# Adding the experts' rows to their tokens by indirect DMA with addition, in place of one-hot products

## The chip, the cores and the metric

The kernel runs on one core of one Trainium2 chip. The metric is device time in microseconds (us) of one execution. The runs before the change took 3098.67 us in the median of three (3094.47 to 3103.86).

## The reference

A two-layer transformer block on 512 tokens of width 1024 with a second, "context" stream of 256 tokens, and then one hybrid layer on the main stream. All is in float32. In each of the two layers both streams pass attention and convolution mixers and then a mixture of 16 experts; the second layer needs the main stream only. The experts choose their tokens:

```python
cap = CAPACITY_FACTOR * t // N_EXPERTS        # 64 rows of the main stream, 32 of the context
gates, idx = lax.top_k(jnp.swapaxes(aff, 1, 2), cap)
xs = jax.vmap(lambda hb, ib: hb[ib])(h, idx)
y = jnp.einsum('becf,efd->becd', jax.nn.silu(a) * u, w_down)
y = y * gates[..., None].astype(y.dtype)
return jax.vmap(lambda ib, yb: jnp.zeros((t, d), yb.dtype).at[ib.reshape(-1)].add(yb.reshape(-1, d)))(idx, y)
```

So every expert's 64 (or 32) output rows of 1024 numbers, times a gate, are added to the tokens that it chose (`x_new + g2 * ...`, with one row of gains g2 for all tokens). A token can be chosen by several experts, and by one expert once.

## The kernel before, in words

The stage that changes is `moe` of the first layer with its loop `experts_two`. A stands for the main stream (4 tiles of 128 tokens, `cap` 64, `dup` 2), B for the context (2 tiles, `cap` 32, `dup` 4). `dup` says how a row of 1024 is cut so that an expert's rows fill 128 partitions: two halves of 512 numbers for A, four quarters of 256 for B.

Before the loop, `out_proj` leaves each stream's rows in on-chip tiles `x` and `xc`; `route_tile` (L1068) norms each tile of 128 tokens, stores it to a tensor `xd` in memory on ScalarE's DMA queue, and works out the routing; `route_turn` leaves, for each expert, a column of row numbers `gi` and a column of gates `ig`.

In the loop over 16 experts, TensorE's instructions stand in the order in which the program writes them (`manual_schedule` over MAN, which is PE); the other engines are ordered by the tile framework. For one expert TensorE does: products of A's gathered rows with the up and gate weights (L1203, 64 instructions), transposes of the next rows of A (L1185), the same products for B (L1203, 128 instructions, on narrower tiles), transposes of the activations (L1224), then the down products of A and of B (L1240, 32 and 64 instructions). The rows are gathered by indirect DMAs on GpSimd (`gather`, L1171) four experts ahead. The weights, 12 entries of 1 MiB for an expert, come on SyncE's DMA queue (L227) into a ring of 13 buffers: an entry is loaded when the buffer that it takes has been read by both streams.

`expert_down` writes the gated rows (down product times gate times g2, on VectorE, L1246) into a tile Y in which the rows of `dup` experts gather: two experts of A or four of B fill it. `combine` (L1249) then adds Y to the tokens: it builds a one-hot matrix from the row numbers on VectorE (L1258), splits Y into a high and a low part (L306 on ScalarE, L307 on VectorE or GpSimd), multiplies with the one-hot matrix on TensorE (L1281: 16 products of 512 columns for A, 8 for B) and adds the result to `x` or `xc` on VectorE (L1284). It is a generator; its pieces are put between the B products of the next expert at the places listed in `PAT` (L1328). The last blocks of both streams have no next expert, and run after the loop. Then `x` stays on chip for the second layer's first norm, and a copy `xsave` is stored to memory, which the second layer reads back later (L980).

`row_bcast` (L388) spreads g2 over all partitions with products (L394) and two copies. In the first expert it does so for A and B, between two groups of weight products. The second layer's loop, `experts_one`, has one stream and calls `combine` with halves of Y. Its first norm (`norm_T`: squares on ScalarE L298, a scale on VectorE, scaled rows L333 and L335, transposes L339) reads `x` directly.

Of the kernel before, what the change touches and what calls it, by code (L numbers as in the profile page):

```python
# [64 lines left out]
CV = 1  # L65
# [24 lines left out]
# columns of the constant array  # L90
# [10 lines left out]
# columns of the row array, read by every partition  # L101
# [12 lines left out]
class Kern:  # L114
# [65 lines left out]
    def load_consts(self):  # L180
# [7 lines left out]
        # sinks negated  # L188
# [28 lines left out]
    def issue(self):  # L217
# [6 lines left out]
        if self.behind is not None:  # L224
            # the load is to queue up behind the rows that are needed before it
# [38 lines left out]
    def rsqrt(self, v, w):  # L264
        """1/sqrt(v) for [128, w], by Newton's steps"""
# [12 lines left out]
    def rsqrt1(self, v):  # L278
        """1/sqrt(v) for [128, 1], by Newton's steps that leave out powers of two until the last"""
# [12 lines left out]
    def rms_scale(self, xs):  # L292
        """per token 1/rms of tiles [128, 1024]"""
# [9 lines left out]
    def split(self, src, hi, lo, eng=None):  # L303
        """hi + lo = src, each with no more bits than one pass carries"""
# [4 lines left out]
    def evac(self, out, in_):  # L309
        """copy out of PSUM, on the two engines in turn"""  # L310
# [12 lines left out]
    def norm_T(self, src, dst, nt, acol, bcol, hi, lo, r=None):  # L323
        """(rms-normed rows)^T * a + b, split, [128 d, 8, tokens]; dst(t) takes the normed rows, hi(k), lo(k) the result"""
# [23 lines left out]
    def mods_steps(self, rounds):  # L348
        """thirds of the modulation vectors, on the partitions; an entry of the stream for each step"""
# [29 lines left out]
    def affine(self, l, m, which):  # L379
        """gain * (1 + scale) on the partitions, for the first (0) or the second (1) norm"""  # L380
# [6 lines left out]
    def row_bcast(self, vec, out, halves=None):  # L387
        """vec [128, 8] on the partitions as a row on every partition"""  # L388
# [27 lines left out]
    def rounds(self, l):  # L416
        """thirds of the modulation that are worked out beside the projections of layer l"""
# [47 lines left out]
    def load_x(self, src, srcc, eng=None):  # L465
        """the residual stream, [128 tokens, tiles, 1024]"""
# [28 lines left out]
    def layer(self, l):  # L495
# [6 lines left out]
        # normed inputs, transposed  # L502
# [60 lines left out]
        # the last layer has room for some of the experts' weights early  # L563
# [15 lines left out]
    def two(self, hT, w, m, n):  # L579
        """two groups of 128 channels"""  # L580
# [9 lines left out]
    def long_conv(self, l, hT, y, sets):  # L590
        """the conformer's convolution"""
# [5 lines left out]
        for ch in range(2):  # L597
            w = self.take_hl(dve=WDVE)
            for m, n in sets:
# [9 lines left out]
                # taps on the vector engine, and (all of the second stream's) on the scalar engine and the pool engine  # L609
# [19 lines left out]
    def channel_norm(self, l, y, sets):  # L629
        """layer norm over the convolution's channels, and silu"""  # L630
# [59 lines left out]
    def att_tiles(self, last):  # L690
        """turned queries of both streams, turned keys of both kinds, and values"""
# [4 lines left out]
    def key_tiles(self):  # L696
        """turned keys of both kinds: the high parts, on both halves of the partitions, and the low ones"""
# [3 lines left out]
    def early_T(self, T, tiles):  # L701
        """the normed inputs turned while the modulation is still on its way, in tiles that attention needs later"""
# [23 lines left out]
    def qkv_group(self, l, hT, last, tiles, W):  # L726
# [85 lines left out]
                # the turning of a tile comes after the products of the next two  # L812
# [13 lines left out]
    def soft(self, ps, n, scale, sink=None, lam=None, pool=None):  # L826
        """softmax of two heads' scores, sink negated; with lam the first less lam times the second"""
# [34 lines left out]
    def pT(self, P, n):  # L862
        """two heads' probabilities transposed: [128 keys, chunks, 2 heads x 128]"""
# [24 lines left out]
    def q_stack(self, q, kind, n):  # L888
        """a block's queries split, the low parts on the other half of the partitions"""
# [9 lines left out]
    def scores(self, out, qs, kT, kv, g, a, b, last=True):  # L899
        """one head's scores of keys a to b"""  # L900
# [71 lines left out]
    def out_proj(self, l, y, T, slots):  # L972
        """x + gate * (y @ w_out), and every tile of it through the second norm and the router"""
# [35 lines left out]
        # by columns first, the first columns' weights make room for the experts'  # L1009
# [3 lines left out]
        for i, t, h in order:  # L1013
# [3 lines left out]
            # the channels that are done last come last  # L1017
# [9 lines left out]
            # the routing of a tile comes after the next products  # L1027
# [21 lines left out]
    def route_init(self, l, m, nt):  # L1049
        """what the router needs: its weights with the gain of the norm in them, and the shift's part of its sums"""  # L1050
# [9 lines left out]
        for k in range(8):  # L1060
# [4 lines left out]
                    xd=self.dram.tile([n, 1024], F32, name=self.nm("xd")),  # L1065
                    wk=[self.one(self.rk, (w,), s=f"wk{m}{w}") for w in (n, 257)], best=[])

    def route_tile(self, l, R, t, x):  # L1068
        """a tile's second norm, stored for the gathers, and its affinities, transposed"""
        nc = self.nc  # L1070
        # the second stream's tiles end beside the first experts, so they take other banks
# [30 lines left out]
        nc.scalar.dma_start(out=R["xd"][t * 128:(t + 1) * 128, :], in_=xs)  # L1102

# [955 lines left out]
```

## Time and profile before

| | |
|---|---|
| time of the runs, median (lowest to highest) | 3098.67 us (3094.47 to 3103.86) |
| profiled execution: span (its only time) | 3111.6 us |
| busy: PE, PEld, DVE, ACT, POOL | 94%, 59%, 45%, 27%, 14% of the span |
| mean granted clock of TensorE | 0.971 |
| DMA | 612.67 MB, mean 197 GB/s |

PE is TensorE's products, PEld its weight loads beside them, DVE VectorE, ACT ScalarE, POOL GpSimd, SP SyncE. The profile's L numbers are the lines of the kernel before. A granted clock of 1.00 is 2.4 GHz, 0.50 is 1.2 GHz. A row of the timeline gives start and length in us, engine, line, operation, the tiles written and read, the number of instructions and, in brackets, idle time before it and what ended it. The first layer's experts lie between about 507 and 1114 us, the second layer's between about 1475 and 1945 us.

### The profile page before, as it was taken

The page shows a single profiled execution, that of the slowest core. Times are in us where ns is not written, and L with a number is a line of the kernel's source. Part 1 is how long each engine was busy: PE and PEld are TensorE (multiplying, and loading weights), DVE is VectorE, ACT ScalarE, POOL GpSimd, SP SyncE. Part 2 cuts the span into 40 slices and gives each one's busy share as a digit, 9 for nine tenths or more (in the row PEclk, how much of TensorE's full clock was granted, in tenths as well). Part 3 has the DMA queues.
Part 4 walks back from the last instruction along what each step waited for, and adds up shares of the span by engine and source line. Part 5 has one row for each costly group of instructions (what it writes and reads, how often), then busy time and mean ns, then how long its engine had stood idle before and what let it go on. Part 6 is the DMA issues. An engine that isn't in the chain of part 4 may idle for free.

```text
span 3111.6 us, 39027 instructions
## 1 busy us (share of the span) xinstructions
PE 2928.2 (94%) x15824; PEld 1831.4 (59%) x15824; DVE 1402.5 (45%) x2893; ACT 847.9 (27%) x1565; POOL 437.2 (14%) x371
## 2 busy tenths in 40 slices
PE   6989999999999989997998888999999999999998
PEld 3556775444444456565332222787887767788786
DVE  4478754232323266765222222642437563354344
ACT  4256431000000143652000000421235442332122
POOL 2224232000000031432000000221210000200000
PEclk9989989999999999898999999999999999999999
DMA  7710126999988844036999999232231112222222
GB/s 269 268 57 14 42 88 248 379 376 359 353 336 338 335 150 177 14 125 235 404 409 409 409 409 390 70 106 84 90 118 62 55 68 81 102 95 95 92 91 75
DMA packets 147236, 612.67 MB, mean 197 GB/s; under 512 B 10416, under 2 KB 10544, under 8 KB 129136
## 3 DMA queue, kind: packets, MB, share of 16 engines
q1 hardware_dynamic: 138272, 580.82, 48.8%
q10 hardware_dynamic: 5040, 17.55, 1.5%
q0 software_dynamic: 3744, 11.81, 1.2%
q8 instruction: 125, 2.05, 0.3%
q14 instruction: 55, 0.45, 0.0%
HBM read 598.60 MB, written 11.53 MB: 196 GB/s over the span
## 4 chain that ended last, share of the span: by engine, by line
PE 70%; DMA 7%; DVE 5%; issue 1%; ACT 1%; POOL 0%; DVEq 0%; POOLq 0%; ACTq 0%
PE pb L1203 11%; PE pd L1240 8%; PE pd L319 7%; PE pd L320 7%; PE pd L321 7%; PE pd L1203 4%; DMA w<-w_up 4%; PE pb L319 3%; PE pb L320 3%; PE pb L321 3%; PE pa L319 3%; PE pa L320 3%; PE pa L321 3%; DMA w<-w_down 2%; PE pb L1281 1%; PE pb L1272 1%
## 5 line engine op out<-in xcount | busy, mean ns | idle before, releaser
L1203 PE MATMUL pb<-w,X 128*64 128x512 f32 x2048 | 466.5, 599 | 26.6 <-DMA w<-w_up 16.6
L1203 PEld LDWEIGHTS pb<-w,X 128*64 128x64 f32 x2048 | 149.2, 137 | 326.4 <-issue 255.7
L258 ACT CAST wh<-w 128x1024 fp32r<-128x1024 f32 (+3 forms) x239 | 236.1, 1029 | 366.2 <-issue 124.6
L1240 PE MATMUL pd<-w,hT 128*64 128x512 f32 (+1 forms) x2048 | 304.3, 494 | 7.9 <-DMA w<-w_down 2.9
L259 DVE TENSOR_TENSOR wl<-w,wh 128x1024 fp32r<-128x1024 f32 (+2 forms) x187 | 229.2, 1244 | 141.4 <-ACT wh L258 136.5
L319 PE MATMUL pd<-hh,wh 128*128 128x512 f32 (+1 forms) x720 | 285.3, 397 | 8.0 <-ACT wh L258 3.3
L321 PE MATMUL pd<-hh,wl 128*128 128x512 f32 (+1 forms) x720 | 283.8, 394 | 0.2 <-DVE wl L259 0.2
L320 PE MATMUL pd<-hl,wh 128*128 128x512 f32 (+1 forms) x720 | 283.5, 394 | 0.0
L259 POOL TENSOR_TENSOR wl<-w,wh 128x1024 fp32r<-128x1024 f32 (+1 forms) x52 | 134.8, 2593 | 482.5 <-ACT wh L258 467.4
L1240 PEld LDWEIGHTS pd<-w,hT 128*64 128x64 f32 (+1 forms) x2048 | 102.5, 124 | 167.4 <-issue 132.0
L1213 ACT ACTIVATE s<-pb 128x512 f32<-128x512 f32 x32 | 19.1, 598 | 640.8 <-PE pb L1203 640.8
L319 PEld LDWEIGHTS pd<-hh,wh 128*128 128x128 f32 x720 | 138.4, 192 | 39.9 <-ACT wh L258 6.3
L321 PEld LDWEIGHTS pd<-hh,wl 128*128 128x128 f32 x720 | 138.1, 192 | 30.0 <-DVE wl L259 1.7
L320 PEld LDWEIGHTS pd<-hl,wh 128*128 128x128 f32 x720 | 138.7, 193 | 27.0 <-issue 0.2
L1191 DVE TENSOR_TENSOR X<-pa,aff 128x512 f32<-128x512 f32 (+1 forms) x48 | 28.9, 602 | 274.8 <-PE pa L1185 274.5
L1246 DVE SCALAR_TENSOR_TENSOR Y<-pd,ig,g 64x512 f32<-64x512 f32 (+1 forms) x128 | 78.7, 615 | 161.7 <-PE pd L1240 160.1
L319 PE MATMUL pb<-wh,fh 128*128 128x512 f32 x352 | 139.3, 400 | 0.8 <-DVE x L1626 0.8
L320 PE MATMUL pb<-wl,fh 128*128 128x512 f32 x352 | 139.3, 396 | 0.0
L321 PE MATMUL pb<-wh,fl 128*128 128x512 f32 x352 | 139.2, 396 | 0.0
L319 PE MATMUL pa<-hh,wh 128*128 128x512 f32 x352 | 139.0, 395 | 0.0
L320 PE MATMUL pa<-hl,wh 128*128 128x512 f32 x352 | 139.0, 395 | 0.0
L321 PE MATMUL pa<-hh,wl 128*128 128x512 f32 x352 | 139.0, 395 | 0.0
(456 smaller groups left out, 4941.4 us busy)
## 6 DMA issues: line engine op xcount, KB each, us to landing
w<-w_up SPq DMA_DIRECT2D x128, 1024.0 KB, 18.5
w<-w_gate SPq DMA_DIRECT2D x128, 1024.0 KB, 12.6
w<-w_down SPq DMA_DIRECT2D x128, 1024.0 KB, 15.9
w<-ada_w SPq DMA_DIRECT2D x48, 1024.0 KB, 6.7
w<-w_in SPq DMA_DIRECT2D x18, 1024.0 KB, 7.7
w<-f1g SPq DMA_DIRECT2D x11, 1024.0 KB, 4.9
w<-f1u SPq DMA_DIRECT2D x11, 1024.0 KB
w<-f2g SPq DMA_DIRECT2D x11, 1024.0 KB, 4.9
```

Source lines behind the costliest of these rows:

```text
L258: nc.scalar.copy(hi[:, s], w[:, s])
L259: (nc.gpsimd if i and not (dve or self.dve) else nc.vector).tensor_tensor(lo[:, s], w[:, s], hi[:, s].bitcast(F32), op=ALU.subtract)
L319: nc.tensor.matmul(ps, lhsT=l[0], rhs=r[0], start=first, stop=False)
L320: nc.tensor.matmul(ps, lhsT=l[0], rhs=r[1], start=False, stop=False)
L321: nc.tensor.matmul(ps, lhsT=l[1], rhs=r[0], start=False, stop=last)
L1191: nc.vector.tensor_tensor(Xv, pv, bc(R["A"]), op=ALU.mult)
L1203: nc.tensor.matmul(pp[h * cap:(h + 1) * cap, 0:w], lhsT=X[:, k], rhs=Wk[:, h * w:(h + 1) * w], start=(k == 0), stop=(k == 7))
L1213: nc.scalar.activation(out=s, in_=pp[:, 0, 0:w], func=AF.Silu)
L1240: nc.tensor.matmul(py[h * cap:(h + 1) * cap, 0:w], lhsT=hT[:, k % nj, k // nj], rhs=Wd[k // 2][:, k % 2, h * w:(h + 1) * w], start=(k == 0 ...
L1246: nc.vector.scalar_tensor_tensor(Y[o:o + cap, h * w:(h + 1) * w], py[sl, 0:w], R["ig"][sl, 16 + e:17 + e], g2[sl, h * w:(h + 1) * w], op0= ...
L1272: nc.tensor.matmul(ps[:, t], lhsT=oh[:, (2 * t2 + t) * 128:(2 * t2 + t + 1) * 128], rhs=z[:, i], start=(i == 0), stop=(i == 1))
L1281: nc.tensor.matmul(ps[:, h * 512:(h + 1) * 512], lhsT=oh[:, t * 128:(t + 1) * 128], rhs=yh[h][:, i], start=(i == 0), stop=(i == 1))
```

## The change

In the first layer the one-hot products go. Each stream gets a tensor `sum` in memory; every tile of tokens is stored there by `route_tile`, in addition to `xd`. Each expert's gated rows are written to a fresh tile Y of 128 partitions in one VectorE instruction per stream (before: one for each half or quarter), and an indirect DMA on GpSimd's queue adds them to the chosen rows of `sum`, with the same row numbers `gi` as the gather. g2 is kept folded in the same way (`fold`). Behind the loop both streams are loaded from `sum` on ScalarE's queue, and `sum` of the main stream takes the place of `xsave`. The second layer keeps its one-hot products; its `combine` loses the branches that it did not use. Comments and docstrings are dropped, too (not shown).

```diff
@@ route_init
+                    sum=self.dram.tile([n, 1024], F32, name=self.nm("sum")) if l == 0 else None,
@@ route_tile
         nc.scalar.dma_start(out=R["xd"][t * 128:(t + 1) * 128, :], in_=xs)
+        if l == 0:
+            nc.scalar.dma_start(out=R["sum"][t * 128:(t + 1) * 128, :], in_=x)
@@ expert_down
-        per = dup
-        o = (e % per) * cap
-        for h in range(dup):
-            sl = slice(h * cap, (h + 1) * cap)
-            nc.vector.scalar_tensor_tensor(Y[o:o + cap, h * w:(h + 1) * w], py[sl, 0:w], R["ig"][sl, 16 + e:17 + e],
-                                           g2[sl, h * w:(h + 1) * w], op0=ALU.mult, op1=ALU.mult)
+        out(py)
+
+    def scatter(self, R, e, g2):
+        nc = self.nc
+        dup = R["dup"]
+        w = 1024 // dup
+        def f(py):
+            Y = self.one(self.yp, (w,), s=f"Y{R['m']}", bufs=2)
+            nc.vector.scalar_tensor_tensor(Y, py[:, 0:w], R["ig"][:, 16 + e:17 + e], g2, op0=ALU.mult, op1=ALU.mult)
+            nc.gpsimd.indirect_dma_start(
+                out=R["sum"].rearrange("t (h w) -> (t h) w", h=dup),
+                out_offset=bass.IndirectOffsetOnAxis(ap=R["gi"][:, e:e + 1], axis=0), in_=Y, in_offset=None, compute_op=ALU.add)
+        return f
+
+    def fold(self, R, row, out):
+        dup, cap = R["dup"], R["cap"]
+        w = 1024 // dup
+        for h in range(dup):
+            sl = slice(h * cap, (h + 1) * cap)
+            self.nc.scalar.copy(out[sl], row[sl, h * w:(h + 1) * w])
@@ experts_two
-            pieces = (None for f in pend for _ in f)
-            pend = []
-            next(pieces, None)
...
+                row = self.one(self.yp, (1024,), s="g2")
                 for r, g in zip(R, g2):
-                    self.row_bcast(self.mod(l, r["m"], 5), g)
+                    self.row_bcast(self.mod(l, r["m"], 5), row)
+                    self.fold(r, row, g)
...
-                if i in PAT:
-                    next(pieces, None)
...
-            self.expert_down(A, e, h0, Wd, Y[0], g2[0], lambda: h1.append(self.expert_T(B, s1)))
-            self.expert_down(B, e, h1[0], Wd, Y[1], g2[1])
+            self.expert_down(A, e, h0, Wd, self.scatter(A, e, g2[0]), lambda: h1.append(self.expert_T(B, s1)))
+            self.expert_down(B, e, h1[0], Wd, self.scatter(B, e, g2[1]))
             self.rel(4)
-            for r in R:
-                if e % r["dup"] == r["dup"] - 1:
-                    pend.append(self.combine(r, e, Y[r["m"]], [self.xc] if r["m"] else self.x, False))
-        return pend
@@ moe
-                pend = self.experts_two(R, g2, l)
+                self.experts_two(R, g2, l)
+            self.xsave = R[0]["sum"]
+            self.load_x(self.xsave, R[1]["sum"])
...
-        if l == 0:
-            self.xsave = self.dram.tile([512, 1024], F32, name="xsave")
-            for t in range(4):
-                nc.scalar.dma_start(out=self.xsave[t * 128:(t + 1) * 128, :], in_=self.xt(t))
```

## Rows read from the trace of the kernel before

**Rows 1.** The page: the span, and busy tenths in 40 slices of it.

```profile
span 3111.6 us, 39027 instructions
...
PE   6989999999999989997998888999999999999998
...
DMA  7710126999988844036999999232231112222222
```

**Rows 2.** Stages: stretch, its us, busy us of five engines, clock, DMA share, GB/s.

```profile
507.70:513.50 5.80, 5.80 (x15) 1.72 (x16) 5.22 (x22) 0.47 (x1) 0.56 (x2) 0.50 0.96 354
549.93:583.67 33.74, 33.74 (x304) 13.81 (x301) 8.38 (x16) 2.81 (x5) 3.11 (x3) 1.00 1.03 408
583.67:622.46 38.79, 38.79 (x320) 16.08 (x316) 11.61 (x17) 1.57 (x3) 2.00 (x3) 1.00 0.90 350
656.20:696.93 40.73, 40.73 (x328) 17.57 (x324) 16.85 (x24) 2.71 (x5) 3.34 (x4) 1.00 0.96 364
549.93:1096.24 546.31, 546.31 (x4634) 226.88 (x4630) 165.55 (x270) 40.51 (x71) 34.53 (x32) 1.00 0.90 349
1096.24:1117.68 21.44, 14.37 (x45) 6.58 (x41) 15.08 (x31) 8.40 (x16) 5.17 (x3) 0.68 0.43 155
1510.00:1860.00 350.00, 306.70 (x1340) 111.19 (x1336) 87.64 (x115) 18.11 (x30) 9.53 (x10) 1.00 1.03 409
```

**Rows 3.** The same for the one-hot products alone (L1281): PE, PEld, then clock.

```profile
549.93:1096.24 546.31, 40.63 (x136) 22.87 (x136) 1.00 0.90 349
```

**Rows 4.** Groups by line and shape, 545 to 1100 us: busy us, mean ns.

```profile
L1246 DVE SCALAR_TENSOR_TENSOR Y<-pd,ig,g 64x512 f32<-64x512 f32 x32 | 24.0, 750 | 42.0 <-PE pd L1240 41.6
...
L1171 POOL DMA_INDIRECT gat<-xd,gi x20 | 19.2, 958 | 279.7 <-PE pa L1185 279.7
```

**Rows 5.** DMA from 537 to 600 us: all; issues, KB, median us to landing.

```profile
DMA packets 6698, 25.68 MB, mean 408 GB/s; under 512 B 441, under 2 KB 441, under 8 KB 6694
...
w<-w_gate SPq DMA_DIRECT2D x5, 1024.0 KB, 15.7
gat<-xd,gi POOLq DMA_INDIRECT x4, 6.2
```

**Rows 6.** Timeline of SyncE: an issue of the weight stream.

```profile
571.44 2.11 SPq L227 DMA_DIRECT2D w<-w_gate  x1
```

**Rows 7.** Timeline of TensorE and ScalarE, first expert.

```profile
507.40 0.37 PE L1098 MATMUL pb<-ct,aff 128*16 128x128 f32 x1 [3.45 <-DVE aff L1095]
...
529.14 1.16 PE L394 MATMUL pa<-ct,mods 128*128 128x128 f32 x8 [1.02 <-DVE g L315]
...
530.13 0.60 PE L1185 MATMUL pa<-ct,gat 128*128 128x128 f32 x4
...
529.15 0.59 ACT L313 COPY g<-pa 128x512 f32<-128x512 f32 x1 [2.24 <-PE pa L394]
```

**Rows 8.** DMA from 440 to 480 us, all queues.

```profile
DMA packets 435, 1.61 MB, mean 40 GB/s; under 512 B 48, under 2 KB 48, under 8 KB 432
```

**Rows 9.** Timeline of TensorE around the end of the last expert.

```profile
1085.12 3.65 PE L1240 MATMUL pd<-w,hT 128*64 128x512 f32 x16
...
1089.07 7.25 PE L1240 MATMUL pd<-w,hT 128*64 128x512 f32 x80
1096.24 0.50 PE L1281 MATMUL pb<-Yh,oh 128*128 128x512 f32 x1
...
1117.68 1.28 PE L339 MATMUL pa<-ct,x 128*128 128x128 f32 x8 [0.22 <-DVE x L335]
```

**Rows 10.** Line L471, loads of a stream's tiles of 512 KB.

```profile
DMA to landing us min/median/max: 3.4/5.2/8.8
```

**Rows 11.** Timeline of ScalarE: the squares and scaled rows behind the experts.

```profile
1111.40 1.06 ACT L298 ACTIVATE junk<-x 128x1024 bf16<-128x1024 f32 x1
1112.36 0.19 ACT L298 ACTIVATION_READ_ACCUMULATOR junk<-x 128x1 f32 x1
...
1117.13 2.56 ACT L333 ACTIVATE x<-x,rsy 128x512 f32<-128x512 f32 x4 [0.85 <-DVE rsy L275]
```

More of the change, by code (lines that the diff above doesn't have):

```diff
@@ L1227, in expert_T, with expert_down @@
         return hT
-    def expert_down(self, R, e, hT, Wd, Y, g2, beside=None):
+    def expert_down(self, R, e, hT, Wd, out, beside=None):
         nc = self.nc
@@ L1258, in combine @@
             nc.vector.tensor_scalar(oh[sl], self.iota[sl, :n], R["ig"][sl, ee:ee + 1], None, op0=ALU.is_equal)
-        yh = []
         for h in range(2):
             c = slice(h * 512, (h + 1) * 512)
-            z = self.one(self.yp, (2, 512), F32R, "Yh", bufs=1 if halves else YHB)
-            self.split(Y[:, c], z[:, 0], z[:, 1], (nc.vector, nc.gpsimd)[h and not (CV and halves)])
-            yh.append(z)
-            if h and not halves:
-                yield
-            if halves or YHB == 1:
-                for t2, xs in enumerate(src):
-                    ps = self.pb((2, 512))
-                    for t in range(2):
-                        for i in range(2):
-                            nc.tensor.matmul(ps[:, t], lhsT=oh[:, (2 * t2 + t) * 128:(2 * t2 + t + 1) * 128], rhs=z[:, i],
-                                             start=(i == 0), stop=(i == 1))
-                    nc.vector.tensor_tensor(xs[:, :, c], xs[:, :, c], ps, op=ALU.add)
-                    yield
-        if not (halves or YHB == 1):
-            for t in range(nt):
-                ps = self.pb()
-                for h in range(2):
+            z = self.one(self.yp, (2, 512), F32R, "Yh", bufs=1)
+            self.split(Y[:, c], z[:, 0], z[:, 1], (nc.vector, nc.gpsimd)[h and not CV])
+            for t2, xs in enumerate(src):
+                ps = self.pb((2, 512))
+                for t in range(2):
                     for i in range(2):
-                        nc.tensor.matmul(ps[:, h * 512:(h + 1) * 512], lhsT=oh[:, t * 128:(t + 1) * 128], rhs=yh[h][:, i],
+                        nc.tensor.matmul(ps[:, t], lhsT=oh[:, (2 * t2 + t) * 128:(2 * t2 + t + 1) * 128], rhs=z[:, i],
                                          start=(i == 0), stop=(i == 1))
-                xs = src[t // 2][:, t % 2]
-                nc.vector.tensor_tensor(xs, xs, ps, op=ALU.add)
+                nc.vector.tensor_tensor(xs[:, :, c], xs[:, :, c], ps, op=ALU.add)
                 yield
     def experts_two(self, R, g2, l):
-        nc = self.nc
         A, B = R
-        Y = [None, None]
-        pend = []
         X = [self.gather_T(A)]
@@ L1296, in experts_two @@
             Wu, Wg = [], []
-            pieces = (None for f in pend for _ in f)
-            pend = []
-            next(pieces, None)
             for k in range(8):
@@ L1327, in experts_two @@
                 self.expert_mm(B, X[1], lambda k: (Wu, Wg)[b][k // 2][:, k % 2], p[:, 1 - b], [k])
-                if i in PAT:
-                    next(pieces, None)
                 if i == TAT:
                     h0 = self.expert_T(A, s0)
-            for _ in pieces:
-                pass
             self.rel(8)
@@ L1400, in moe @@
         ey = self.phase(yp=1)
-        self.iota = self.one(self.yp, (512,), s="iota")
-        nc.gpsimd.iota(self.iota, pattern=[[1, 512]], base=0, channel_multiplier=0, allow_small_or_imprecise_dtypes=True)
-        g2 = [self.one(self.yp, (1024,), s=f"g2{r['m']}") for r in R]
+        if l == 1:
+            self.iota = self.one(self.yp, (512,), s="iota")
+            nc.gpsimd.iota(self.iota, pattern=[[1, 512]], base=0, channel_multiplier=0, allow_small_or_imprecise_dtypes=True)
+        g2 = [self.one(self.yp, (1024 if l == 1 else 1024 // r["dup"],), s=f"g2{r['m']}") for r in R]
         MARK("experts")
@@ L1423, in moe @@
             with self.tc.manual_schedule(engines={getattr(mybir.EngineType, n) for n in MAN}) if MAN else nullcontext():
-                pend = self.experts_two(R, g2, l)
+                self.experts_two(R, g2, l)
+            self.xsave = R[0]["sum"]
+            self.load_x(self.xsave, R[1]["sum"])
         else:
             pend = self.experts_one(R[0], g2[0], l)
-        with self.prio(CPRI[l]):
-            for f in pend:
-                for _ in f:
-                    pass
+            with self.prio(CPRI[l]):
+                for f in pend:
+                    for _ in f:
+                        pass
         self.xslots = None
```

18 lines of the change are left out of this document (12 added, 6 removed).

## The prediction, made before the change was run

> **What bounds the kernel now.** I read the page's 40 slices first [rows 1]: in slices 8 to 14, the first layer's experts, TensorE is busy nine tenths or more throughout, and the DMA engines nearly as much. Then the stage table [rows 2]: over 546.3 us, from the second expert's start to the last expert's end, TensorE has 546.31 us of work at clock 1.00. It never waits, so whatever leaves its queue there leaves the time, as long as nothing else comes to the limit. The same table shows the next limit. An expert without one-hot products takes 33.74 us and the DMA engines run at 408 GB/s in it, as fast as in the second layer's experts (409 GB/s), where TensorE does wait. So two resources stand almost level, and the question is how much the new transfers add to the second.
>
> **What is removed.** Three rows of the stage table are the three kinds of expert: 33.74 us without one-hot products, 38.79 with those of the main stream (5.05 more), 40.73 with both streams' (6.99 more). Inside the stretch the one-hot line has 136 products [rows 3]: seven main-stream blocks of 16 and three context blocks of 8. That is four experts of +5.05 and three of +6.99: 20.2 + 21.0 = 41.2 us. The splits, the one-hot rows and the additions on VectorE, ScalarE and GpSimd lay beside TensorE's work and bring nothing of their own. The eighth and fourth blocks come behind the last expert and belong to the boundary, below.
>
> **What the scatters cost inside the loop.** Each expert now ends with two indirect DMAs that add 128 rows of 2 KB and 128 rows of 1 KB: 0.39 MB, the same bytes that it gathers. On GpSimd each should take about 1 us, as a gather does [rows 4]; the scatter waits for VectorE's product, and behind it on GpSimd's queue stand only gathers for four experts later (some 135 us), so nobody waits for them. A scatter must also wait for the one before it on the same tensor; a gather lands 6.2 us after its issue [rows 5], a fifth of an expert, so this wait is over long before.
> The price is in transfer time. An expert moves 12 MiB of weights and 0.39 MB of gathered rows, 12.98 MB, at 408 GB/s [rows 5] 31.8 us; against 33.74 us that leaves 1.9 us per expert. Call S the transfer time of an expert's two scatters. Beyond 1.9 us every microsecond of S is paid by 14 experts, after the ring's lead is used up. That lead: the last gate load of the next expert is issued at 571.44 [rows 6], lands some 15.7 us later [rows 5], at 587.1, and is needed when three quarters of the first 13.95 us of the expert that starts at 583.67 are done, at 594.1: 7 us. So the loss is 14 x (S - 1.9) - 7 us where that is positive.
> No row shows an adding DMA. From below: moved once like the gathers, 0.39 MB at 408 GB/s is 1.0 us, loss 0. From above: if the engines could do nothing else until both had landed, 2 x 6.2 = 12.4 us, loss 140 us. An addition in memory has to fetch the old row and write the new one, so I take two moves, S = 1.9, loss 0: nearer to the gather, because gathers of the same rows already run among the weights at undiminished 408 GB/s. It just fits; this is the weakest term, and both ends stay in the range.
> The Trainium skill ("DMA: Bandwidth & Descriptors", Rules for kernel authors) states that an accumulating DMA reads its destination and writes it later, and that the next access of those bytes has to wait for its semaphore. By that rule S would be two moves, as taken; with one move the sum would be the same, since both fit into the 1.9 us. The traces here show only the one-way gather.
>
> **The first expert.** The gate row is now broadcast into one buffer for both streams, and copied from there in 2 and 4 pieces on ScalarE. The second stream's broadcast waits until the two copies of the first are done. TensorE's next transposes stand right behind the broadcast products [rows 7], so two copies, each at most the 0.59 us of the 128-partition copy in the same rows, come on top: 1.2 us. The 6 new stores of 512 KB to the sum tensors are 1.3 us each at 408 GB/s; four fall into a time when the DMA queues are nearly empty (40 GB/s) [rows 8], two beside the first expert's loads. I take +2 us together; bounds 0 and +5.
>
> **The boundary to the second layer.** Now: from the last down product (1096.24) to the first transposes of the next norm (1117.68) it is 21.4 us [rows 9], with two blocks of one-hot products in it. After: the chain starts where the main stream's last down product ends, and the context's follows it. Of the last 80 products in 7.25 us, 16 are the main stream's, at 3.65/16 = 0.23 us each [rows 9]: 3.6 us, so the context's 64 take the other 3.6. From the main stream's end: 0.3 for a semaphore (an estimate), gating product 0.75 [rows 4], semaphore 0.3, scatter issued and landed 6.2 [rows 5], four loads of 512 KB 3.4 for the first and 1.3 for each further one [rows 10], 7.3; last square with its accumulator 1.25, then 4.6 from its end to the first scaled rows and 0.55 until transposes start [rows 11]. Sum 21.3, less the 3.6 that lie beside the context's product: 17.7 us, 3.7 less than now. Against it: TensorE is now idle for nearly all of that, where it had one-hot products in pieces at a mean clock of 0.68. In the first expert, behind a wait of 3.45 us [rows 7], the clock stood at 0.50 (1.2 GHz) for the next 5.8 us [rows 2]; 5.8 us at half clock cost 2.9 us, less here, where vector work paces the transposes. I take -2 us in all. Bounds: -6 (loads together, scatter at once) and +9 (scatter twice as long, loads at the 8.8 us of [rows 10]).
> The Trainium skill ("DMA: Bandwidth & Descriptors", Anatomy of one DMA) fits a GpSimd-issued DMA at 2.0 us plus bytes over 436 GB/s, 2.6 us for 256 KB; the trace's gathers of that size take 6.2 between full weight queues, and the measurement decides. By the page the sum would be 3.6 us lower.
>
> **Sum.** -41.2 + 0 + 2 - 2 = -41 us on the profiled execution, of which only the span of 3111.6 us is known: 3070. The timed runs have a median of 3098.67, 12.9 us below that span, all of them under it; taken off the median the forecast is 3058 us.
>
> **The rivals.**
> 1. The transfers become the bound, but mildly. For it: 408 GB/s in an expert of 33.74 us is full speed already, and a row of 1 or 2 KB that is read and rewritten may well need more than two moves. Against it: seven experts of 16 had 5 to 7 us of one-hot products and the mean there is 349 GB/s [rows 2], which shows room only in those. At S = 3.5 the loss is 14 x 1.6 - 7 = 15 us: 3073 us.
> 2. The boundary takes longer: what was in on-chip memory has to be written, awaited and read back, at the +9 end in place of -2. 3069 us. Against it: the lead of 3.6 us, and that the old path also had splits, products and additions in series.
> 3. Slower. The adding scatter holds the DMA engines row by row: fetch, add, write, with the weights behind it. Each engine has 16 rows per expert. At S = 8 us (0.5 us a row) the loss is 14 x 6.1 - 7 = 78 us: 3136 us. It decides from S = 5.3 us, 0.33 us a row, where the 41 us are used up. For it: no row excludes it, and the loads have no lead left to hide it. Against it: the gathers' rows, as small, cost no bandwidth.
> That the change would not do what it says I give no weight: the 160 products leave the first layer by the diff.
>
> **How the numbers follow.** My forecast, with S up to 2.5 and the boundary near its value, has chance 0.52; the longer boundary 0.10; mild transfer bound (S 2.5 to 4.4, up to 28 us lost) 0.18; S between 4.4 and 5.8, which lands within 0.3% (9.3 us, about what a measurement of this kernel can tell from no change), 0.07; S above 5.8 0.13. Faster 0.80, same 0.07, slower 0.13. Likeliest case alone: 3049 to 3067. The range runs from 3049 (boundary at -6 and the first expert at 0, with the runs' spread) to 3095, S = 5 us, beyond which some 0.17 lies.
>
> **What would show it.** Right: experts 2 to 15 take 33.7 us each, TensorE without idle time before weight products, DMA at 409 GB/s nearly throughout, no one-hot products before the second layer, the last down product some 41 us earlier, adding scatters whose packets take about twice a gather's. S wrong: TensorE's idle time in front of the weight products, ended by weight loads, equal per expert, and periods above 34 us. Boundary wrong: more than 21 us from the last down product to the transposes, ended by loads of the stream. The forecast as a whole is wrong if the periods exceed 36 us.

## The result, and the profile after

The changed kernel takes 3068.74 us (3058.08 to 3070.44), the kernel before in the same series 3100.43 (3094.47 to 3103.86): ratio 0.9888, 95% interval 0.9874 to 0.9902. Two more series of both gave 0.9879 (0.9858 to 0.9900) and 0.9886 (0.9871 to 0.9901), that is 32, 40 and 36 us. The forecast was -41 us, 3058. The page of the changed kernel answers to [rows 1]; its profiled execution was timed at 3069.82 us:

```profile
span 3068.0 us, 38600 instructions
...
PE   6989998999999899996998888999999999999998
...
DMA  7710126999999843057999998222231112222222
```

TensorE stays at nine tenths through the first layer's experts, while the DMA's row has lost what room it had there. The table by stretches answers to [rows 2]: the second expert, from its start to the last down product, the boundary.

```profile
544.92:578.67 33.75, 33.75 (x306) 13.82 (x302) 4.64 (x9) 1.57 (x3) 5.19 (x4) 1.00 1.03 397
544.92:1052.41 507.49, 505.91 (x4502) 206.28 (x4502) 70.44 (x133) 27.41 (x49) 70.84 (x52) 1.00 1.01 387
1052.41:1075.89 23.48, 8.52 (x41) 0.81 (x32) 3.37 (x16) 5.83 (x11) 3.71 (x2) 0.61 0.97 356
```

The loop went from 546.31 to 507.49 us. For the first time TensorE waits in it: 507.49 less 505.91 busy is 1.6 us. The boundary row is the surprise. It is 2 us longer than before, TensorE is busy for 8.5 us of 23.5, and the DMA engines, at a share of 0.43 before, are at 0.97.

The two waits in the loop, in the timeline of TensorE:

```profile
759.79 2.79 PE L1206 MATMUL pb<-w,X 128*64 128x512 f32 x12 [0.79 <-DMA w<-w_gate]
...
895.76 2.80 PE L1206 MATMUL pb<-w,X 128*64 128x512 f32 x12 [0.75 <-DMA w<-w_gate]
```

The group of weight products between 545 and 1100 us, with busy us, mean ns, and the idle time before them with what ended it:

```profile
L1206 PE MATMUL pb<-w,X 128*64 128x512 f32 x960 | 210.0, 594 | 1.6 <-DMA w<-w_gate 1.5
```

Both end with a load of gate weights, the load whose lead the prediction counted. Eleven of the fourteen periods from expert 1 to expert 15 are 33.74 us to 0.05; the others, of experts 4, 7 and 11, are 34.00, 34.75 and 34.71.

What answers to [rows 4], groups of GpSimd and VectorE by shape in the same stretch:

```profile
L1270 POOL DMA_INDIRECT sum<-Y,gi x31 | 49.8, 1606 | 219.8 <-DVE Y L1269 217.9 <-DMA w<-w_gate 1.8 <-issue 0.2
L1174 POOL DMA_INDIRECT gat<-xd,gi x20 | 20.0, 1000 | 195.9 <-PE pa L1188 195.9
...
L1269 DVE SCALAR_TENSOR_TENSOR Y<-pd,ig,g 128x512 f32<-128x512 f32 x15 | 11.3, 751 | 45.9 <-PE pd L1243 45.9
```

A scatter holds GpSimd 1.6 us, not the 1 us taken from the gather; nobody waits for it in the loop. And what answers to [rows 5], the DMA from 578 to 952 us, eleven experts; q0 is the queue of GpSimd's gathers and scatters, with its packets, MB and share of the 16 engines, and an issue line ends with the median us to landing:

```profile
DMA packets 40638, 148.23 MB, mean 396 GB/s; under 512 B 2774, under 2 KB 4182, under 8 KB 40608
...
q0 software_dynamic: 4320, 7.87, 9.1%
...
sum<-Y,gi POOLq DMA_INDIRECT x22, 8.0
gat<-xd,gi POOLq DMA_INDIRECT x18, 5.7
```

The timeline of the changed kernel around the end of the last expert (SPq and ACTq are SyncE's and ScalarE's queues):

```profile
1040.48 32.00 SPq L227 DMA_DIRECT2D w<-ada_w  x6
...
1045.17 7.25 PE L1243 MATMUL pd<-w,hT 128*64 128x512 f32 x80
...
1049.90 2.28 POOL L1270 DMA_INDIRECT sum<-Y,gi  x1 [3.64 <-DVE Y L1269]
...
1054.73 1.56 POOL L1270 DMA_INDIRECT sum<-Y,gi  x1 [0.16 <-issue]
...
1055.37 2.02 ACTq L471 DMA_DIRECT2D x<-sum  x4
...
1059.38 1.94 PE L358 MATMUL pb<-w,sT 128*32 128x512 f32 x8 [6.11 <-DMA w<-ada_w]
...
1064.20 0.81 ACTq L475 DMA_DIRECT2D xc<-sum  x2
...
1065.06 1.06 ACT L298 ACTIVATE junk<-x 128x1024 bf16<-128x1024 f32 x1 [19.35 <-DMA x<-sum]
...
1071.41 1.06 ACT L298 ACTIVATE junk<-x 128x1024 bf16<-128x1024 f32 x1 [1.69 <-DMA x<-sum]
...
1075.89 0.69 PE L339 MATMUL pa<-ct,x 128*128 128x128 f32 x2
```

The four loads of x are issued at 1055.37, 5.5 us after the issue of the scatter that they wait for. The last of them is only used at 1071.41, 16.0 us later, where the prediction had 7.3. Beside them SyncE streams the `ada_w` tiles, weights of the modulation products (L358), which TensorE turns to meanwhile.

### The profile page after: what moved, and what is told of

Read it like the earlier page. It is cut to its first block, busy times and chain, and to the rows that moved or that the text cites. A ratio compares the mean times of both kernels' runs of the same rounds, so it can differ in the third digit from the quotient of the medians.

```text
span 3068.0 us, 38600 instructions
## 1 busy us (share of the span) xinstructions
PE 2874.2 (94%) x15664; PEld 1800.9 (59%) x15664; DVE 1298.4 (42%) x2745; ACT 835.8 (27%) x1547; POOL 472.3 (15%) x390
## 3 DMA queue, kind: packets, MB, share of 16 engines
HBM read 601.74 MB, written 18.87 MB: 202 GB/s over the span
## 4 chain that ended last, share of the span: by engine, by line
PE 53%; DMA 7%; DVE 4%; ACT 1%; issue 0%; SPq 0%; ACTq 0%; DVEq 0%; POOLq 0%
PE pd L319 7%; PE pd L321 7%; PE pd L320 7%; DMA w<-w_up 4%; PE pb L1206 4%; PE pd L1243 3%; PE pb L319 3%; PE pb L320 3%; PE pb L321 3%; PE pa L319 3%; PE pa L320 3%; PE pa L321 3%; DMA w<-w_down 3%; PE pb L1301 1%; PE pa L872 1%; PE pa L883 1%
## 5 line engine op out<-in xcount | busy, mean ns | idle before, releaser
L258 ACT CAST wh<-w 128x1024 fp32r<-128x1024 f32 (+3 forms) x239 | 235.9, 1029 | 362.7 <-issue 124.3
L259 DVE TENSOR_TENSOR wl<-w,wh 128x1024 fp32r<-128x1024 f32 (+2 forms) x187 | 231.0, 1253 | 140.2 <-ACT wh L258 135.5
L259 POOL TENSOR_TENSOR wl<-w,wh 128x1024 fp32r<-128x1024 f32 (+1 forms) x52 | 134.2, 2580 | 429.4 <-ACT wh L258 424.8
L1174 POOL DMA_INDIRECT gat<-xd,gi x48 | 46.9, 977 | 544.4 <-PE pa L1188 290.1
```

What stands on the lines that cost most here:

```text
L258: nc.scalar.copy(hi[:, s], w[:, s])
L259: (nc.gpsimd if i and not (dve or self.dve) else nc.vector).tensor_tensor(lo[:, s], w[:, s], hi[:, s].bitcast(F32), op=ALU.subtract)
L1174: self.nc.gpsimd.indirect_dma_start(out=g, out_offset=None, in_=R["xd"].rearrange("t (h w) -> (t h) w", h=dup), in_offset=bass.IndirectOff ...
```

## The experiments

Besides the time, each profiled execution was cut at the same marks of TensorE, read from its timeline: expert 0's first weight product; the loop from expert 1's start to the last down product's end; from expert 15's start to the first transpose of the norm (L339) and to the last product of the next step (L802; in e9_lastdep the two lines are L345 and L808); and from there to the second layer's first weight product. All in us; the median of the timed runs last.

| kernel | expert 0 at | loop | to first L339 | to last L802 | to second layer | median |
|---|---|---|---|---|---|---|
| before | 507.7 | 546.4 | 54.2 | 149.7 | 259.8 | 3100.4 |
| before, again | 503.9 | 546.4 | 54.0 | 149.2 | 256.0 | 3103.3 (one run) |
| changed | 504.0 | 507.5 | 56.3 | 150.5 | 260.0 | 3068.7 |
| changed, e1_again | 499.0 | 507.4 | 57.3 | 150.2 | 253.5 | 3063.3 |
| changed, e5_again2 | 503.6 | 508.1 | 56.4 | 152.8 | 253.5 | 3067.2 |
| e2_nohot | 503.5 | 505.2 | 52.9 | 147.6 | 254.9 | 3052.8 |
| e3_plain | 501.8 | 505.2 | 57.6 | 151.1 | 256.0 | 3063.5 |
| e4_twice | 500.6 | 529.1 | 57.0 | 153.4 | 253.5 | 3088.5 |
| e6_spload | 500.2 | 507.8 | 50.1 | 148.3 | 259.7 | 3064.3 |
| e7_nolast | 503.8 | 515.0 | 40.0 | 134.4 | 259.6 | 3049.4 |
| e8_lastchip | 504.1 | 508.8 | 49.4 | 145.9 | 254.5 | 3061.9 |
| e9_lastdep | 500.6 | 508.2 | 49.9 | 147.8 | 254.9 | 3065.5 |

Two columns scatter whatever the kernel: expert 0's start, by up to 9 us, and the stretch to the second layer, near 260 in four rows and 253.5 to 256.0 in the others. So a change is read from the loop and from the way to the last L802; medians of different series compare to a few us only.

**The price of adding rows.** Four kernels, one series. The changed kernel as it is:

> The changed kernel itself, once more, beside the other runs of this series. The profiled executions differ by 43.6 us (3111.6 to 3068.0), the medians by 31.7. If the profiled execution of before was a long one of its kind (3111.6 us lies above all its four timed runs), the difference here is 32 to 37 us, ratio 0.988 to 0.990. If the stages' differences are all real (5 us of them lie ahead of the second expert), it is 40 to 44 us, ratio 0.986 to 0.987.

The kernel before with its one-hot products left out of the loop and nothing in their place, so that the rows of the earlier experts are missing from x:

```diff
-                if e % r["dup"] == r["dup"] - 1:
+                if e == 15:
                     pend.append(self.combine(r, e,
```

> The kernel before, with the first layer's one-hot products left out except those of the last expert: the rows of experts 1 to 15 are not added to their tokens. No scatter, no store of the sums, the boundary as before. If TensorE's queue bounded the loop, the loop alone gives back 41.2 us: second expert to last down product 505 us in place of 546.3, every expert 33.7 us, TensorE without waits, time 3100 - 41 = 3059 us. If the gain of the change came from the vector engines' work or from the boundary, less than 20 us.

The changed kernel with scatters that overwrite where they should add, so that the sums are not the sums any more:

```diff
             nc.gpsimd.indirect_dma_start(
                 out=R["sum"].rearrange("t (h w) -> (t h) w", h=dup),
-                out_offset=bass.IndirectOffsetOnAxis(ap=R["gi"][:, e:e + 1], axis=0), in_=Y, in_offset=None, compute_op=ALU.add)
+                out_offset=bass.IndirectOffsetOnAxis(ap=R["gi"][:, e:e + 1], axis=0), in_=Y, in_offset=None)
```

> The changed kernel with scatters that write their rows instead of adding them (the additions are left out, a token keeps the last expert's row). Price theory: an adding row of 2 KB takes 176 ns of a DMA engine and one of 1 KB 101 ns, which makes S = 2.2 us per expert; plain rows should take about half, 85 and 45 ns, S = 1.1 us; the 2.3 us of waits for weights in the loop go, the loop is 505 us, and the time is 2 to 5 us under the changed kernel's. Rival: the price is per row and not the addition's; then packets and waits stay and the time does not move.

And the changed kernel with a second adding scatter, of zeros, behind each but the last expert's:

```diff
                 out_offset=bass.IndirectOffsetOnAxis(ap=R["gi"][:, e:e + 1], axis=0), in_=Y, in_offset=None, compute_op=ALU.add)
+            if e < 15:
+                nc.gpsimd.indirect_dma_start(
+                    out=R["sum"].rearrange("t (h w) -> (t h) w", h=dup),
+                    out_offset=bass.IndirectOffsetOnAxis(ap=R["gi"][:, e:e + 1], axis=0), in_=self.zero[:, 0:w],
+                    in_offset=None, compute_op=ALU.add)
```

> The changed kernel, and behind each scatter of experts 1 to 15 a second one of the same size that adds a tile of zeros to the same rows, so S doubles to 4.4 us per expert. If transfer time beyond 1.9 us per expert is paid once the ring's 7 us are used up, the loop loses 14 x (4.4 - 1.9) - 7 = 28 us where it lost 2.3 before: time 24 to 28 us over the changed kernel's, experts of 36 us each, waits in front of the weight products ended by weight loads, DMA at full rate throughout. Rival (scatters go beside the weights for nothing, the 2.3 us of waits have another cause): time within 5 us of the changed kernel's.

The medians were 3063.32, 3052.82, 3063.51 and 3088.49 us (before in this series: 3103.0); ratios 0.9879 (0.9858 to 0.9900), 0.9835 (0.9820 to 0.9850), 0.9876 (0.9861 to 0.9891) and 0.9960 (0.9945 to 0.9975). First the loop. Without any scatter, and with plain ones, it is the same to the hundredth and TensorE never waits: in both kernels, e2_nohot first, then e3_plain, span and busy time agree:

```profile
544.36:1049.57 505.21, 505.21 (x4499) 206.54 (x4495) 105.41 (x200) 28.24 (x51) 21.92 (x22) 1.00 0.96 377
```

```profile
543.05:1048.26 505.21, 505.21 (x4502) 206.74 (x4502) 70.40 (x133) 27.38 (x49) 52.97 (x52) 1.00 0.98 389
```

That is the 546.3 - 41.2 = 505.1 us of the prediction. The addition alone, then, costs the changed kernel's loop 507.5 - 505.2 = 2.3 us: 1.6 us of waits, and 0.7 by which its products count as busy for longer. Its transfer time S comes from the share of q0 between 578 and 952 us, where every one of these kernels issues 18 gathers. The share of e2_nohot, gathers alone; of e3_plain; and of e4_twice:

```profile
q0 software_dynamic: 1152, 3.54, 3.1%
```

```profile
q0 software_dynamic: 2640, 8.13, 5.9%
...
sum<-Y,gi POOLq DMA_INDIRECT x23, 6.2
```

```profile
q0 software_dynamic: 7343, 12.06, 15.3%
...
sum<-zero,gi POOLq DMA_INDIRECT x22, 7.9
sum<-Y,gi POOLq DMA_INDIRECT x21, 8.2
```

Plain scatters: 5.9 - 3.1 = 2.8% of 374 us is 10.5 us for 23 scatters, 0.91 us per expert (a pair). Adding ones: 9.1 - 3.1 = 6.0%, 22.4 us for 22, 2.04 us per pair. Twice as many: 12.2%, 45.6 us for 43, 2.12 per pair. These differences take the gathers to cost the same in every kernel, but one of their 4 KB packets takes 211 ns in e2_nohot and 171 in the changed kernel. The packets of the added rows themselves give a little more: 176 ns for a row of 2 KB and 101 ns for one of 1 KB, each row in a packet of its own, 128 of each on 16 engines: 2.2 us per pair. A plain pair goes in 96 packets of 4 KB, 175 ns each (the gathers' among them), 1.05 us. Either way an added row takes 2.1 to 2.2 times the transfer time of a written one.

e3_plain leaves out the addition and with it the small packets, so that the two are not told apart by a run. Smaller packets alone hardly explain the price: from the added row of 1 KB to that of 2 KB it grows by 75 ns, where 1 KB of a plain packet takes 44. The Trainium skill ("DMA: Bandwidth & Descriptors", Rules for kernel authors) states that an accumulating DMA reads its destination and writes it later. The time agrees with two moves, 2.04 against 0.91 us; the read itself no run shows, since the bytes that the pages count as read are 601.74 MB in the changed kernel, in e3_plain and in e4_twice alike.

The law of the prediction, 14 x (S - 1.9) - 7, gives 25 us for the doubled scatters with S = 4.2, and 28 with the 4.4 that the expectation took; the loop of e4_twice is 529.1 - 505.2 = 23.9 us above the ideal, and the median 25.2 above e1_again's. TensorE's waits there are the named ones (us in all, times, longest), from 541 to 1070 us:

```profile
PE pb L1206 <- DMA w<-w_gate: 17.8, 11, 3.1
```

They make 17.8 of the 23.9 us. The other 6.1 are products that took longer, as the row of the loop shows (busy 511.3 us, clock 0.99; between 740 and 780 us, where the longest wait lies, the clock is 0.96):

```profile
541.78:1070.90 529.12, 511.30 (x4502) 205.81 (x4502) 70.07 (x133) 27.48 (x49) 117.96 (x82) 0.99 1.03 383
```

The periods were expected at 36 us each and are uneven, 33.7 to 40.0.

So the scatters of the change about fill an expert's room for transfers: a plain pair costs the loop nothing, an adding pair 2.3 us, two of them 23.9. The law has the size right and not the shape. For S = 2.04 (or 2.2) it gives nothing and 2.3 us were lost, and from one pair to two it would add 14 us for each us of S beyond the room, some 31 us, where 21.6 were found. So neither the room of 1.9 us nor the lead of 7 us is measured, and why the late loads fall on experts 4, 7 and 11 the runs do not show.

The median of e2_nohot lies 50 us under the kernel before, where 41 were expected, and 10.5 us under e1_again's. The loop gives 2.2 of it and the way to the last L802 2.6; the rest isn't found in these marks, and the profiled spans (3057.4 and 3055.3 us) don't show it. Nor does e3_plain's median show the 2.2 us that its loop gains, and the 2 to 5 us expected of it. e1_again lies 39.7 us under the kernel before, ratio 0.9879, between the two cases of its expectation; the last run below decides between them.

**The boundary.** Three kernels and the changed one as their base, one series.

> The changed kernel once more, as the base of this series: 3060 to 3068 us; 23 to 25 us from the end of the last down product to the first transpose of the attention norm, and 150 to 151 us from the start of expert 15 to the last product of L802, as in its two profiled executions so far.

The reload on SyncE's queue, in line with the `ada_w` loads and no longer beside them:

```diff
-            self.load_x(self.xsave, R[1]["sum"])
+            self.load_x(self.xsave, R[1]["sum"], nc.sync)
```

> The reload of x and xc from memory is issued on SP's queue, in order with the loads of the ada weights, instead of on ScalarE's. Theory A (the first layer's end is late because the reload shares the DMA engines with the ada loads issued before and beside it): the loads that SP would issue after it wait, the reload lands some 7 us earlier, the stretch from the last down product to the first transpose goes from 24 to about 17 us and the time falls by about 5 us. Rival B (the ada products that TensorE does meanwhile are due anyway, and set the end together with the norm): the ada products come later by what the norm gains, expert 15 to the last L802 stays at 150 us, and the time at 0 to +5 us, the more so as SP now stands in front of the ada loads until the last scatter has landed.

The reload at the start of expert 15, whose rows are left out of the sums:

```diff
             pp = self.expert_ps(A)
+            if e == 15:
+                self.xsave = A["sum"]
+                self.load_x(A["sum"], B["sum"])
...
+            if e == 15:
+                return
             nc.gpsimd.indirect_dma_start(
                 out=R["sum"].rearrange("t (h w) -> (t h) w", h=dup),
```

> The scatters of expert 15 are left out (its rows miss in the sums), and x and xc are loaded back at the start of expert 15, while it computes: what the wait for the last scatter and the reload cost at most. Theory A: x is there when the last down product ends, the first transpose follows within 5 to 8 us in place of 24, expert 15 to the last L802 goes from 150 to 135 to 140, and the time falls by 12 to 17 us. Rival B: the ada products fill that stretch already, so that expert 15 to the last L802 falls by under 4 us and the time by 0 to 4.

The same reload, with the rows of expert 15 added on the chip by one-hot products, and to the main stream's `sum` in memory, too, for its later readers:

```diff
+    def finish(self, R, e, Y, src):
...
+            oh = self.one(self.yp, (n,), F32R, f"oh{R['m']}{h}", bufs=1)
+            nc.vector.tensor_scalar(oh, self.iota[:, :n], own[:, h:h + 1], None, op0=ALU.is_equal)
...
+        self.split(Y, z[:, 0], z[:, 1], nc.vector)
...
+                    nc.tensor.matmul(ps[:, h * w:(h + 1) * w], lhsT=ohs[h][:, t * 128:(t + 1) * 128], rhs=z[:, i],
+                                     start=(i == 0), stop=(i == 1))
+            nc.vector.tensor_tensor(xs, xs, ps, op=ALU.add)
```

> As the one before in that x and xc are loaded back at the start of expert 15, but its rows are added to them on the chip by one-hot products, as the kernel before did for each expert (the 24 products of 8 and 4 tiles, with masks, and a scatter for the copy of x that stays in memory). Theory A: the first transpose 11 to 13 us after the last down product, since the products take some 9 to 16 us at either clock; expert 15 to the last L802 some 140 to 143 us; the time 8 to 12 us under the changed kernel's. Rival B: what the norm gains the ada products lose: within 3 us of the changed kernel; and the reload in the loop takes 1.5 MB of a DMA that is 93% busy, which makes expert 15 late by up to 3.7 us, so perhaps slower.

The medians were 3067.19 (base), 3064.27, 3049.38 and 3061.92 us; ratios 0.9886 (0.9871 to 0.9901), 0.9867 (0.9852 to 0.9882), 0.9826 (0.9813 to 0.9840) and 0.9864 (0.9849 to 0.9879).

The base came to 152.8 us to the last L802, outside its expected 150 to 151, so that this mark scatters by some 2.5 us in the changed kernel itself.

e6_spload splits the question in two. Its loads of x landed 8.0 us after their issue:

```profile
x<-sum SPq DMA_DIRECT2D x4, 512.0 KB, 8.0
```

The first transpose came 17.3 us after the last down product, in place of 23.5: the part of theory A on where the reload lost its time was right, to the number. But the last L802 came only 2 to 4.5 us earlier, and the median is 2.9 lower, with overlapping intervals. TensorE's waits from the last down product to the last L802 say why, in the changed kernel:

```profile
PE pb L358 <- DMA w<-ada_w: 16.4, 5, 6.1
```

and in e6_spload:

```profile
PE pa L339 <- DVE x L335: 8.0, 1, 8.0
PE pb L358 <- DMA w<-ada_w: 8.0, 3, 6.4
```

The wait was dealt out otherwise, 16.0 in place of 16.4 us. Both the norm and the modulation products have to be done before the next step ends, and in this stretch what they wait for, the `ada_w` tiles and the reloaded rows, comes over DMA engines with a share of 0.97. Their bytes, from 1049 to 1076 us in the changed kernel (q1 the weights, q10 the reload; packets, MB, share):

```profile
q1 hardware_dynamic: 659, 4.87, 45.8%
q10 hardware_dynamic: 864, 3.15, 28.7%
q0 software_dynamic: 288, 0.39, 10.6%
```

3.15 MB are 7.7 us at 408 GB/s, and the order in which they go changes little. So theory A was right on the reload, B on the mark that follows; the time lies between A's 5 us gained and B's 0 to 5 lost.

e7_nolast takes the bytes out of that stretch. The same list of waits has for it

```profile
PE pb L358 <- DMA w<-ada_w: 1.6, 1, 1.6
```

and the last L802 comes 16 us earlier than in the changed kernel (134.4 against 150.5; 18 against the base), the median 17.8 under the base, a little more than theory A had. That is what waiting for the last scatter and reading the stream back cost together; the run does not tell the two apart. It is no upper bound, since the reload's squares stood ahead of expert 15's activation on ScalarE and TensorE waited 5.8 us behind it, so that the loop took 515.0.

e8_lastchip keeps the whole computation and gets about a third of it: 145.9 to the last L802, 4 to 7 us less than the changed kernel's three executions, and 5.3 us under the base by the medians, between the two theories. Its median is the lowest of a whole kernel here, but its interval overlaps the changed kernel's and e6_spload's, so that the gain rests on the profile's marks. It has 32 added products, not the 24 of the expectation. The first transpose came 16.0 us after the last down product, not 11 to 13; the timeline shows where the rest went:

```profile
1052.04 1.23 DVE L259 TENSOR_TENSOR wl<-w,wh 128x1024 fp32r<-128x1024 f32 x1 [5.45 <-ACT wh L258]
1053.19 0.74 DVE L1270 SCALAR_TENSOR_TENSOR Y<-pd,ig,g 128x512 f32<-128x512 f32 x1
...
1055.02 0.49 PE L1331 MATMUL pb<-Yh,oh 128*128 128x512 f32 x1 [1.12 <-ACT Yh L306]
1057.41 4.36 PE L1331 MATMUL pb<-Yh,oh 128*128 128x512 f32 x11 [1.90 <-DVE Yh L307]
...
1065.78 1.92 PE L358 MATMUL pb<-w,sT 128*32 128x512 f32 x16
```

Splits of the next weights (L258, L259) stand ahead of the last rows on VectorE and ScalarE. The next run held them back behind those rows.

```diff
+        if self.first:
+            z = self.first.pop()
+            for k in (0, n):
+                nc.scalar.copy(hi[:, k, 0:1], z[:, 1, 0:1])
```

> As the kernel that adds the last expert's rows on the chip, and besides the casts of the attention weights w_in on ScalarE, and with them VectorE's splits, are held until the last expert's rows are split, so that they no longer stand ahead of them on the two engines. Theory A (the norm is late by what stood ahead of the rows: 1.1 and 1.9 us of waits between the added products): the first transpose comes 12 to 13.5 us after the last down product in place of 16.0, expert 15 to the last L802 some 143 to 145 us in place of 145.9, the time 3058 to 3061 us. Rival B (the w_in products follow the transposes at once, so that a late cast costs what the early rows gain): expert 15 to the last L802 within 1 us of 145.9, or longer, and the time 3061 to 3065.

It gained nothing: 3065.52 us, ratio 0.9885 (0.9869 to 0.9902), 147.8 to the last L802, the interval overlapping e8_lastchip's. The added products did start at once and took 7.7 us in place of 10.8, but the first transpose still came 16.2 us after the last down product. The held splits now stood in the norm's own chain on VectorE, and an instruction of the context's norm there that takes 0.17 us elsewhere took 2.31, while GpSimd ran its share of the splits (L265, from 1063.68 for 2.34 us):

```profile
1060.63 0.16 DVE L306 TENSOR_SCALAR v<-ss 128x4 f32<-128x4 f32 x1
...
1062.12 1.23 DVE L265 TENSOR_TENSOR wl<-w,wh 128x1024 fp32r<-128x1024 f32 x1
...
1063.74 2.31 DVE L276 TENSOR_SCALAR rsy<-rst 128x2 int32<-128x2 int32 x1
...
1066.16 1.67 DVE L341 TENSOR_SCALAR x<-x,rsy 128x512 f32<-128x512 f32 x4
```

5.5 us from the mean of squares to the scaled rows, where e8_lastchip takes 2.4. The marks are those of rival B, though by another cause than the one it named; the time lies just above its range.

**The kernel before, once more.**

> The kernel before, profiled once more, to tell what of the differences between the two first profiled executions belongs to the change. Theory A (the 5.0 us by which expert 1 began earlier after the change are the clock's, not the change's): expert 0 starts between 499 and 508 us here too, and by 0 to 8 us before the 507.7 of the first execution; the stretch from the start of expert 1 to that of expert 15 is 513.5 us within 0.5, and the span is nearer to the timed median, 3095 to 3105 us. Rival B (the change itself brings the first expert forward, through the loads that it leaves out): expert 0 starts again at 507 to 508.

One run of 3103.27 us, span 3101.5. Expert 0 began at 503.9, as in the changed kernel, and the loop was the same as in the first execution to the hundredth. Theory A: what the changed kernel seemed to gain ahead of the experts (507.7 against 504.0) is not the change's, so that e1_again's first case, the long execution of the kernel before, is the one that holds.

## Why the prediction was right, and where it was off

**What bounds the loop: right.** TensorE bound it, one-hot work was its only price, and the transfers were next and came just level. 546.38 to 507.49 us, -38.9, against -41.2 + 0; without scatters, e2_nohot, the -41.2 come out as worked out.

**S, the weakest term: nearly right.** Taken as two moves, 1.9 us; measured 2.04 to 2.2. It was a choice between bounds of 1.0 and 12.4 us, with no row of an adding DMA, so that its closeness is in part luck. The loss taken at 0 is 2.3 us. Rival 1 named the mechanism of this loss, at 15 us; e4_twice shows it at work, with 24 us at S = 4.2 to 4.4. Rival 3, slower from S = 5.3 us, is excluded by S itself. One sign was named differently than it came: a packet of an added 2 KB row takes 176 ns, as long as a gather's of 4 KB (171), so the price is double by bytes and not by packets. And one bin of the chances is misplaced: by its own law S = 4.4 still leaves a gain of 13 us, and a result within 9.3 us of no change would need S from 4.7 to 6.0. The scatter's landing, 8.0 us and not 6.2, and its issue, 1.6 us and not 1, were off but stand beside other work.

**The first expert: +2 taken, about 0 found.** The time from expert 0 to expert 1 is 42.2 and 40.7 us before, 40.9, 41.8 and 40.4 after. Neither the fold's copies nor the stores show beyond that scatter. This error and the loop's 2.3 us cancel, which is luck.

**The boundary: the step that failed.** 17.7 us were forecast from the last down product to the first transpose, 23.5 found (24.4 and 23.5 in the two repeats), which is the prediction's own sign for a wrong boundary. The term is the reload's: 7.3 us from issue to the last landing, built from [rows 10], was 16.0, because the `ada_w` stream behind the experts starts as soon as buffers come free and shares the engines; ahead of most of that stream, in e6_spload, the loads landed after 8.0. The 3.4 us of [rows 10] belong to a load at 398.7 us, in a stretch where the DMA share was 0.44 (398 to 412 us), not the 0.97 of this one. The other terms came out 2.9 us shorter together (scatter 5.5 us from issue to the loads' issue, and 4.5 from the start of the last square to the transposes, where 6.4 were taken). The sum also left out the modulation products: TensorE is not idle for nearly all of the stretch but does 40 of the 128 in it, 16 before the change.

That is rival 2, given 0.10, with another cause than its own bound had, since the scatter was not late, and not at its price: +9 was its boundary. Its 3069 us being the measured median is a coincidence.

And the mark does not set the time by itself: in e6_spload the first transpose came 6 us earlier and the time hardly moved. To the last L802, where norm and modulation products have met, it is 149.7 and 149.2 us before, 150.5, 150.2 and 152.8 after, so the boundary lost 1 to 3 us. Forecast -2.

**The sum.** -38.9 in the loop, 0 at the first expert, +1 to +3 at the boundary: -36 to -38 us, between the 32, 40 and 36 us of the three series. The forecast of 3058 also started from a median of three runs, 3098.67; the later series have 3100 to 3103 for the same kernel. The scatter of the series has one visible source: from the last L802 to the second layer the same instructions take 260.0 us in one execution of the changed kernel and 253.5 in another, at granted clocks of 0.89 and 0.93, as the rows of the changed kernel and of e1_again show.

```profile
1170.03:1430.04 260.01, 227.63 (x1097) 159.83 (x1097) 171.98 (x393) 125.35 (x231) 79.92 (x59) 0.89 0.30 112
```

```profile
1165.55:1419.07 253.52, 220.94 (x1097) 156.51 (x1097) 172.04 (x394) 125.44 (x231) 79.91 (x59) 0.93 0.31 115
```

The 43.6 us between the first two profiled spans were too many: the span before, 3111.6, was itself 10 us longer than that of e9_before2.

## What to carry to other kernels

Work moved from an engine to DMA cost some twice the transfer time of plain rows here, where rows are added in memory; compare that with the free transfer time of one loop turn, and check it by doubling the transfer. The price of keeping the sum in memory shows less in the loop (2.3 us here) than at its end (16 us between the changed kernel and e7_nolast), where the last scatter, the reload and the prefetch of the next stage meet on the same engines; take a load's landing time from a stretch that is as full as the one it will stand in. And measure a boundary at the point where all branches join, since the first late instruction may only change places with another.

## What was not expected of the hardware

- An adding scatter occupied GpSimd 1.61 us and landed after 8.0 us; the same scatter without the addition took 1.01 us and landed after 6.2, like a gather (1.00 us, 5.7). GpSimd's groups in e3_plain, 545 to 1100 us:

```profile
L1270 POOL DMA_INDIRECT sum<-Y,gi x30 | 30.3, 1009 | 228.2 <-DVE Y L1269 225.7 <-DMA w<-w_up 2.4 <-issue 0.2
```

- With the scatters added, the DMA engines moved 397 GB/s in an expert where they had moved 408 [rows 2], at the same share of 1.03: an added row of 2 KB takes an engine as long (176 ns) as a gather's packet of 4 KB (171).
